# Two decoder layers with a mixture of experts: TensorE's products of the experts' stage pinned to the order of the program

## Chip, cores and metric

One NeuronCore of a Trainium2 chip runs the whole program in one launch. The metric is the device time of one execution in microseconds. A second, profiled execution gives the trace; all stretches below are counted from the start of its span.

## What is computed

512 tokens of width 1024 go through two layers. Each layer has a dense part (norm, one wide projection, three mixers, gated merge, output projection) and then a mixture of experts. A router picks one of four groups and two of its eight experts for each token; all 32 experts of the layer run on the tokens that chose them. The experts' stage is what matters here:

```python
g_sel = jnp.argmax(g_logits, axis=-1)
top_v, top_i = lax.top_k(e_logits, TOP_K)
weights = jax.nn.softmax(top_v, axis=-1) * p_group
...
def expert_block(args):
    xb, e = args
    return (jax.nn.silu(xb @ w_exp_gate[e]) * (xb @ w_exp_up[e])) @ w_exp_down[e]
...
y_rows = y_rows.astype(F32) * row_w[:, None]
out = jax.ops.segment_sum(y_rows, row_tok, num_segments=n_tok + 1)[:n_tok]
```

## The kernel before

`body` runs `dense(l)` and then `moe(l)` for the two layers. In `moe` (from L1059) every expert has a place for 64 tokens (`CAP`). The outer loop runs over eight groups `g` of four experts, the inner loop over two pairs `q` of each group. What TensorE does for a pair, in the order in which the program writes it:

- `expert_up` (L1303) makes the gate and up products of one expert. The 64 tokens' activations are the stationary operand, so a product fills 64 of the array's 128 columns; the two halves `j` of the result go to the two column halves, in turn. One expert is 16 products, which the trace shows as 32 matmuls; it reads four weight blocks of 1 MiB.
- `expert_mid` (L1313) has no large product. ScalarE takes the SiLU (L1317), VectorE multiplies (L1318), TensorE transposes the result in two pieces (L1321) and ScalarE copies it out (L1323). Its tile `h` has one buffer.
- `expert_slots` (L1326) transposes the one-hot matrix of the pair (L1332) and makes the routing weights of its slots (L1336).
- `expert_down` (L1343) makes the down products of both experts of the pair, expert `j` in column half `j`, again in turn (32 matmuls, L1350, four weight blocks). VectorE scales the result (L1356), ScalarE and VectorE split it in two parts (L1357, L1358).
- `back` (L1362) adds the scaled rows back to the tokens: products of a full-width one-hot with both parts (L1371), and a VectorE addition into `x` for each (L1374).
- `gather` (L1277) collects the four experts' tokens of a group: eight parts of eight full-width matmuls (L1290), each copied out by ScalarE (L1292).

The program spreads these over the pairs. In pair `q` = 0 it writes: up of the first expert, half of `back` for the group before, `expert_mid`, up of the second, the other half of `back`, `expert_slots`, `expert_mid`, `expert_down`. In `q` = 1 it writes: two ups, `expert_mid`, `expert_slots`, four parts of the next group's gather, `expert_mid`, `expert_down`, four more parts. Groups 3 and 7 end differently: they have no gather ahead, and `back` follows at once. Between groups 3 and 4 a loop (`extra`, L1428) serves experts with more than 64 tokens.

The weights come through `fetch` (L1170): one transfer of 1 MiB for each block, all issued by SyncE's queue in the order of use, into a ring of twelve places in the first layer and thirteen in the second (nine around the extra loop). A transfer waits until TensorE has finished with the block that had the place before.

The order of instructions on each engine is not written by hand. When the program is built, a scheduler goes through its own estimate of when each instruction's operands are ready and lets each engine take what is ready; the order of the program decides only among those. Data dependencies always hold. PSUM has two buffers for the up products (`mm`), two for the down products (`rt`) and four for everything else (`sm`).

Of the kernel before, what the change touches and what calls it, by code (L numbers as in the profile page):

```python
# [9 lines left out]
F32 = mybir.dt.float32  # L10
# [10 lines left out]
NT = S // 128  # L21
# [154 lines left out]
class Kern:  # L176
# [16 lines left out]
    def c(self, name):  # L193
        o, n = CW[name]
        n1 = CW["i2"][0]
        return self.consts[0][:, o:o + n] if o < n1 else self.consts[1][:, o - n1:o - n1 + n]
# [994 lines left out]
    def route(self, op, rp, lg):  # L1191
# [82 lines left out]

        return pos, late

    def gather(self, oh, n, ahead=3):  # L1277

        nc = self.nc
        l, x, a, b, g2b, xh, xl = self.env  # L1280
        xg = self.xgp.tile([128, 8, 4 * CAP], F32, tag="xg", name="xg")[:, :, :n]
        made = [0]

        def part(k):
            pg = self.psum()[:, :n]
            po = pg.rearrange("p (a s) -> p a s", s=oh.shape[-1])
            i = 0
            for src in (xh, xl):
                for t in range(NT):
                    nc.tensor.matmul(po if len(oh.shape) == 4 else pg, src[:, t, k * 128:(k + 1) * 128], oh[:, t], start=i == 0, stop=i == 7)  # L1290
                    i += 1
            nc.scalar.activation(xg[:, k], pg, AF.Identity, scale=a[:, k:k + 1], bias=b[:, k:k + 1])  # L1292

        def get(k):
            while made[0] < min(8, k + ahead):
                part(made[0])
                made[0] += 1
            return xg[:, k]

        get(0)  # L1300
        return get

    def expert_up(self, xg, wgu):  # L1303

        nc = self.nc
        ph = self.psum("mm")
        for k in range(8):
            for j in range(2):
                nc.tensor.matmul(ph[64 * j:64 * j + 64].rearrange("p (u f) -> p u f", u=2), xg(k),  # L1309
                                 wgu(k)[:, :, 256 * j:256 * j + 256], start=k == 0, stop=k == 7)  # L1310
        return ph

    def expert_mid(self, ph):  # L1313

        nc, c, mp = self.nc, self.c, self.mp
        h = mp.tile([128, 256], F32, tag="h", name="h")
        nc.scalar.activation(h, ph[:, :256], AF.Silu)  # L1317
        nc.vector.tensor_tensor(h, h, ph[:, 256:], op=OP.mult)  # L1318
        pt = self.psum()[:, :256]
        for q in range(2):  # L1320
            nc.tensor.transpose(pt[:, q * 128:(q + 1) * 128], h[:, q * 128:(q + 1) * 128], c("ident"))  # L1321
        hT = mp.tile([128, 2, 2, CAP], F32, tag="hT", name="hT", bufs=3)
        nc.scalar.activation(hT.rearrange("p q j s -> p (q j s)"), pt, AF.Copy)  # L1323
        return hT

    def expert_slots(self, oh, wcol):  # L1326

        nc, c, mp = self.nc, self.c, self.mp
        ohT = mp.tile([128, S], F32R, tag="ohT", name="ohT", bufs=2)
        pt = self.psum()  # L1330
        for t in range(NT):
            nc.tensor.transpose(pt[:, t * 128:(t + 1) * 128], oh[:, t].bitcast(F32), c("ident"))  # L1332
        nc.scalar.activation(ohT, pt, AF.Copy)
        pw = self.psum()
        for t in range(NT):
            nc.tensor.matmul(pw[:, :4], oh[:, t], wcol(t), start=t == 0, stop=t == NT - 1)  # L1336
        ws = self.misc.tile([128, 1], F32, tag="ws", name="ws", bufs=2)
        for j in range(2):
            js = slice(64 * j, 64 * j + 64)
            nc.vector.tensor_reduce(ws[js], pw[js, 2 * j:2 * j + 2], axis=AX.X, op=OP.add)  # L1340
        return ohT, ws

    def expert_down(self, hT, wd, ohT, ws):  # L1343

        nc, g2b = self.nc, self.env[4]
        pys = [self.psum("rt") for _ in range(2)]
        for f in range(4):
            for n in range(2):
                for j in range(2):
                    nc.tensor.matmul(pys[n][64 * j:64 * j + 64], hT[j][:, f % 2, f // 2], wd(j, f)[:, 512 * n:512 * n + 512],  # L1350
                                     start=f == 0, stop=f == 3)
        ys = []
        for n in range(2):
            yh, yl = (self.parts.tile([128, 512], F32R, tag=tag, name=tag, bufs=4) for tag in ("yh", "yl"))
            y = pys[n]
            nc.vector.scalar_tensor_tensor(y, y, ws, g2b[:, n * 512:(n + 1) * 512], op0=OP.mult, op1=OP.mult)  # L1356
            nc.scalar.activation(yh, y, AF.Copy)  # L1357
            nc.vector.tensor_tensor(yl, y, yh.bitcast(F32), op=OP.subtract)  # L1358
            ys.append((yh, yl))
        return ohT, ys  # L1360

    def back(self, done, last=False, blocks=range(NT)):  # L1362

        nc, x = self.nc, self.env[1]
        for t in blocks:
            for n in range(2):
                px = self.psum()
                i = 0
                for ohT, ys in done:
                    for y in ys[n]:  # L1370
                        nc.tensor.matmul(px, ohT[:, t * 128:(t + 1) * 128], y, start=i == 0, stop=i == 2 * len(done) - 1)  # L1371
                        i += 1
                xs = x[:, t, n * 512:(n + 1) * 512]
                nc.vector.tensor_tensor(xs, xs, px, op=OP.add)  # L1374
                if last:
                    nc.scalar.activation(px, xs, AF.Square, accum_out=self.ssx[:, n, t:t + 1])  # L1376
# [162 lines left out]
```

## Time and profile before

| what | value |
|---|---|
| time, median of 3 runs (lowest, highest) | 2514.08 us (2507.03, 2515.6) |
| the profiled execution's own time | 2514.72 us |
| its span, first to last instruction | 2512.9 us |
| PE busy | 2348.6 us, 93% of the span |
| weight loads of TensorE (PEld) busy | 1581.0 us, 63% |
| DVE, ACT busy | 1121.0 us (45%), 657.8 us (26%) |
| matmuls of L1309 and of L1350 with the ring's weights | 2048 and 1024 |
| read from HBM | 568.58 MB |

A group of instructions is named by its line, engine and operation, with the tile that it writes and those that it reads. A matmul's duration in the trace is longer than the distance to the next one, since they overlap; distances are therefore taken from start to start. A bracket at the end of a row of the timeline is the idle time of that engine just before it, and what ended it.

### The profile page before, as it was taken

What the parts mean: (1) busy time and instruction counts of PE and PEld (TensorE: products, weight loads), DVE (VectorE), ACT (ScalarE), POOL (GpSimd) and SP (SyncE); (2) the same over time, 40 slices, a digit from 0 to 9 for tenths busy, and PEclk for the clock granted to TensorE, in tenths of its full rate; (3) what the DMA queues carried; (4) which work ended last, traced back from release to release, by engine and by line L of the source; (5) the groups of instructions that cost most, each with busy time, mean ns of one, the idle gap of its engine ahead of it and who ended that gap; (6) DMA issues with size and microseconds to landing.
All of it is one profiled execution on the core that took longest, in us unless ns stands there. A gap on an engine that the chain in (4) does not pass through costs nothing. (4 is left out here: it accounts for less than half of the span.)

```text
span 2512.9 us, 35831 instructions
## 1 busy us (share of the span) xinstructions
PE 2348.6 (93%) x14542; PEld 1581.0 (63%) x14542; DVE 1121.0 (45%) x2569; ACT 657.8 (26%) x1126; POOL 7.4 (0%) x26
## 2 busy tenths in 40 slices
PE   6999999999979998999989999999999899999997
PEld 4777778777945444554457777787779454445443
DVE  7648665874332122222246477568543322212213
ACT  4323324223321111111143233342233221111111
POOL 0000000000000000000000000000000000000000
PEclk9999999999989999999999999999999899999999
DMA  7222335775459996799942322268453699799993
GB/s 291 63 79 68 86 105 186 258 256 199 150 227 414 360 353 269 323 421 353 347 155 71 85 68 69 100 194 272 161 182 145 239 412 364 302 384 420 394 375 146
DMA packets 139949, 587.22 MB, mean 234 GB/s; under 512 B 37381, under 2 KB 39685, under 8 KB 90629
## 3 DMA queue, kind: packets, MB, share of 16 engines
q1 hardware_dynamic: 136608, 576.44, 61.7%
q10 hardware_dynamic: 3172, 8.45, 1.0%
q8 instruction: 116, 1.90, 0.3%
q14 instruction: 53, 0.43, 0.0%
HBM read 568.58 MB, written 12.06 MB: 231 GB/s over the span
## 5 line engine op out<-in xcount | busy, mean ns | idle before, releaser
L1309 PE MATMUL ps_mm<-w_at,xg_at 128*64 128x512 f32 x2048 | 482.7, 599 | 0.0
L346 PE MATMUL ps_mm<-hTh_at,whi_at 128*128 128x512 f32 x1024 | 414.1, 404 | 10.3 <-DVE b_at L964 4.1
L346 PE MATMUL ps_mm<-hTh_at,wlo_at 128*128 128x512 f32 x1024 | 409.7, 400 | 10.9 <-DVE wlo_at L218 10.9
L346 PE MATMUL ps_mm<-hTl_at,whi_at 128*128 128x512 f32 x1024 | 409.2, 400 | 0.0
L1309 PEld LDWEIGHTS ps_mm<-w_at,xg_at 128*64 128x64 f32 x2048 | 164.5, 136 | 223.6 <-issue 213.0
L217 ACT ACTIVATE whi_at<-raw_at 128x1024 fp32r<-128x1024 f32 (+1 forms) x180 | 170.1, 946 | 471.0 <-PE ps_mm L346 382.5
L218 DVE TENSOR_TENSOR wlo_at<-raw_at,whi_at 128x1024 fp32r<-128x1024 f32 (+1 forms) x180 | 193.9, 1079 | 170.6 <-ACT whi_at L217 157.9
L1350 PE MATMUL ps_rt<-w_at,hT_at 128*64 128x512 f32 x1024 | 253.1, 598 | 0.0
L346 PEld LDWEIGHTS ps_mm<-hTh_at,wlo_at 128*128 128x128 f32 x1024 | 195.7, 191 | 61.9 <-DVE wlo_at L218 18.0
L346 PEld LDWEIGHTS ps_mm<-hTh_at,whi_at 128*128 128x128 f32 x1024 | 195.6, 191 | 53.7 <-issue 7.1
L346 PEld LDWEIGHTS ps_mm<-hTl_at,whi_at 128*128 128x128 f32 x1024 | 195.8, 191 | 43.9 <-issue 4.7
L1356 DVE SCALAR_TENSOR_TENSOR ps_rt<-ps_rt,ws_at,g2b_at 128x512 f32<-128x512 f32 x66 | 50.0, 758 | 280.4 <-PE ps_rt L1350 277.2
L1350 PEld LDWEIGHTS ps_rt<-w_at,hT_at 128*64 128x64 f32 x1024 | 99.4, 136 | 103.1 <-issue 89.2
L1318 DVE TENSOR_TENSOR h_at<-h_at,ps_mm 128x256 f32<-128x256 f32 x65 | 27.3, 421 | 305.8 <-ACT h_at L1317 305.6
L1374 DVE TENSOR_TENSOR x_at<-x_at,ps_sm 128x512 f32<-128x512 f32 x136 | 90.0, 685 | 130.7 <-PE ps_sm L1371 130.4
L1292 ACT ACTIVATE xg_at<-ps_sm,mod_at,mod_a_at 128x256 f32<-128x256 f32 x136 | 76.8, 565 | 181.5 <-PE ps_sm L1290 181.2
L312 DVE SCALAR_TENSOR_TENSOR w_ada_at<-w_ada_at,crow_at 128x1024 f32<-128x1024 f32 x80 | 97.7, 1222 | 52.7 <-DMA w_ada_at<-in_w_ada_dram 52.2
L1371 PE MATMUL ps_sm<-yh_at,ohT_at 128*128 128x512 f32 x264 | 105.9, 415 | 5.7 <-ACT yh_at L1357 3.5
L1371 PE MATMUL ps_sm<-yl_at,ohT_at 128*128 128x512 f32 x264 | 104.2, 411 | 0.4 <-DVE yl_at L1358 0.4
L1317 ACT ACTIVATE h_at<-ps_mm 128x256 f32<-128x256 f32 x65 | 24.9, 384 | 302.6 <-PE ps_mm L1309 302.6
L1290 PE MATMUL ps_sm<-oh_at,xh_at 128*128 128x256 f32 x512 | 95.4, 302 | 6.8 <-DVE oh_at L1105 2.9
L1290 PEld LDWEIGHTS ps_sm<-oh_at,xh_at 128*128 128x128 f32 x512 | 74.3, 198 | 40.3 <-issue 40.3
(373 smaller groups left out, 2995.1 us busy)
## 6 DMA issues: line engine op xcount, KB each, us to landing
w_at<-in_w_exp_dram SPq DMA_DIRECT2D x256, 1024.0 KB, 9.7
w_at<-in_w_down_dram SPq DMA_DIRECT2D x128, 1024.0 KB, 8.1
raw_at<-in_w_in_dram SPq DMA_DIRECT2D x84, 512.0 KB, 3.7
w_ada_at<-in_w_ada_dram SPq DMA_DIRECT2D x80, 512.0 KB, 4.4
raw_at<-in_w_gate_dram SPq DMA_DIRECT2D x48, 512.0 KB, 4.4
raw_at<-in_w_branch_dram SPq DMA_DIRECT2D x48, 256.0 KB, 3.9
w_ada_at<-in_w_ada_dram SPq DMA_DIRECT2D x8, 1024.0 KB, 12.8
raw_at<-in_w_o_dram SPq DMA_DIRECT2D x16, 512.0 KB, 4.8
```

Source lines behind the costliest of these rows:

```text
L217: nc.scalar.activation(hi, src, AF.Copy)
L218: (eng or nc.vector).tensor_tensor(lo, src, hi.bitcast(F32), op=OP.subtract)
L312: nc.vector.scalar_tensor_tensor(w, w, 1.0, self.crow, op0=OP.mult, op1=OP.mult, accum_out=m)
L346: self.nc.tensor.matmul(ps, w[a][:, k], x[b][:, k], start=n == 0, stop=n == last)
L1290: nc.tensor.matmul(po if len(oh.shape) == 4 else pg, src[:, t, k * 128:(k + 1) * 128], oh[:, t], start=i == 0, stop=i == 7)
L1292: nc.scalar.activation(xg[:, k], pg, AF.Identity, scale=a[:, k:k + 1], bias=b[:, k:k + 1])
L1309: nc.tensor.matmul(ph[64 * j:64 * j + 64].rearrange("p (u f) -> p u f", u=2), xg(k), wgu(k)[:, :, 256 * j:256 * j + 256], start=k == 0, st ...
L1318: nc.vector.tensor_tensor(h, h, ph[:, 256:], op=OP.mult)
L1350: nc.tensor.matmul(pys[n][64 * j:64 * j + 64], hT[j][:, f % 2, f // 2], wd(j, f)[:, 512 * n:512 * n + 512], start=f == 0, stop=f == 3)
L1356: nc.vector.scalar_tensor_tensor(y, y, ws, g2b[:, n * 512:(n + 1) * 512], op0=OP.mult, op1=OP.mult)
L1371: nc.tensor.matmul(px, ohT[:, t * 128:(t + 1) * 128], y, start=i == 0, stop=i == 2 * len(done) - 1)
L1374: nc.vector.tensor_tensor(xs, xs, px, op=OP.add)
```

## The change

`Kern` gets two helpers, `mm` and `turn`. They issue a matmul or a transpose and hand it to `keep_in_program_order` of the framework. This ties the instruction behind the last one that was written for the same engine in the same block of the program: an edge of order for the scheduler, without a semaphore and without a wait on the chip. All matmuls and transposes of `gather`, `expert_up`, `expert_mid`, `expert_slots`, `expert_down` and `back` go through the helpers, and since `extra` calls these functions, its products do as well. The order of the other engines' instructions and of the transfers is left to the scheduler. No operand, tile, buffer or count of instructions is changed.

```diff
+    def mm(self, *a, **k):
+
+        self.tc.keep_in_program_order(self.nc.tensor.matmul(*a, **k))
+
+    def turn(self, *a, **k):
+        self.tc.keep_in_program_order(self.nc.tensor.transpose(*a, **k))
...
-                    nc.tensor.matmul(po if len(oh.shape) == 4 else pg, src[:, t, k * 128:(k + 1) * 128], oh[:, t], start=i == 0, stop=i == 7)
+                    self.mm(po if len(oh.shape) == 4 else pg, src[:, t, k * 128:(k + 1) * 128], oh[:, t], start=i == 0, stop=i == 7)
...
-                nc.tensor.matmul(ph[64 * j:64 * j + 64].rearrange("p (u f) -> p u f", u=2), xg(k),
+                self.mm(ph[64 * j:64 * j + 64].rearrange("p (u f) -> p u f", u=2), xg(k),
...
-            nc.tensor.transpose(pt[:, q * 128:(q + 1) * 128], h[:, q * 128:(q + 1) * 128], c("ident"))
+            self.turn(pt[:, q * 128:(q + 1) * 128], h[:, q * 128:(q + 1) * 128], c("ident"))
...
-            nc.tensor.transpose(pt[:, t * 128:(t + 1) * 128], oh[:, t].bitcast(F32), c("ident"))
+            self.turn(pt[:, t * 128:(t + 1) * 128], oh[:, t].bitcast(F32), c("ident"))
...
-            nc.tensor.matmul(pw[:, :4], oh[:, t], wcol(t), start=t == 0, stop=t == NT - 1)
+            self.mm(pw[:, :4], oh[:, t], wcol(t), start=t == 0, stop=t == NT - 1)
...
-                    nc.tensor.matmul(pys[n][64 * j:64 * j + 64], hT[j][:, f % 2, f // 2], wd(j, f)[:, 512 * n:512 * n + 512],
+                    self.mm(pys[n][64 * j:64 * j + 64], hT[j][:, f % 2, f // 2], wd(j, f)[:, 512 * n:512 * n + 512],
...
-                        nc.tensor.matmul(px, ohT[:, t * 128:(t + 1) * 128], y, start=i == 0, stop=i == 2 * len(done) - 1)
+                        self.mm(px, ohT[:, t * 128:(t + 1) * 128], y, start=i == 0, stop=i == 2 * len(done) - 1)
```

## Rows read from the trace of the kernel before

**Rows 1.** The page: its head, the busy times, and the largest group (out<-in, count, busy us, mean ns of one).

```profile
span 2512.9 us, 35831 instructions
PE 2348.6 (93%) x14542; PEld 1581.0 (63%) x14542; DVE 1121.0 (45%) x2569; ACT 657.8 (26%) x1126; POOL 7.4 (0%) x26
L1309 PE MATMUL ps_mm<-w_at,xg_at 128*64 128x512 f32 x2048 | 482.7, 599 | 0.0
```

**Rows 2.** Busy times by stretch; the stretches run from the first up product of a second pair (`q` = 1) to that of the next, or to the end of the last `back`. Columns: stretch, its length, busy us and count of PE, PEld, DVE, ACT and POOL, granted TensorE clock, DMA share, GB/s.

```profile
740.99:803.39 62.40, 62.40 (x317) 34.38 (x315) 14.86 (x29) 10.75 (x22) 0.00 (x0) 1.00 1.01 416
803.39:872.45 69.06, 65.19 (x315) 32.07 (x313) 14.70 (x29) 11.18 (x22) 0.00 (x0) 1.00 0.94 365
...
941.51:976.26 34.75, 32.06 (x143) 15.55 (x139) 14.54 (x39) 4.73 (x10) 0.00 (x0) 1.00 0.91 361
1048.72:1113.31 64.59, 64.58 (x317) 33.29 (x314) 14.85 (x29) 10.75 (x22) 0.00 (x0) 1.00 1.01 420
...
1251.45:1287.88 36.43, 32.62 (x143) 15.54 (x140) 13.23 (x26) 9.71 (x22) 1.07 (x2) 1.00 0.51 193
1995.66:2058.03 62.37, 62.37 (x317) 34.36 (x315) 14.87 (x29) 10.75 (x22) 0.00 (x0) 1.00 1.01 416
2058.03:2125.50 67.47, 65.14 (x314) 32.42 (x312) 14.69 (x29) 11.18 (x22) 0.00 (x0) 1.00 0.96 369
...
2194.56:2229.34 34.78, 32.09 (x143) 15.56 (x139) 12.52 (x23) 4.52 (x9) 0.00 (x0) 1.00 0.93 389
2261.55:2326.14 64.59, 64.58 (x316) 33.29 (x314) 14.85 (x29) 10.75 (x22) 0.00 (x0) 1.00 1.01 421
...
2395.20:2464.27 69.07, 65.20 (x315) 32.05 (x312) 13.23 (x25) 11.18 (x22) 0.00 (x0) 1.00 0.95 368
2464.27:2500.42 36.15, 32.49 (x143) 15.45 (x139) 11.00 (x19) 8.45 (x21) 0.00 (x0) 1.00 0.19 72
```

**Rows 3.** Timeline of PE from 742.28 to 803.39 us of the span, one row for each of nine places in it. Columns: start us, us, engine, line, operation, out<-in, shape, count.

```profile
742.28 14.01 PE L1309 MATMUL ps_mm<-w_at,xg_at 128*64 128x512 f32 x61
756.22 0.44 PE L1321 MATMUL ps_sm<-consts_at,h_at 128*128 128x128 f32 x2
...
761.53 7.86 PE L1350 MATMUL ps_rt<-w_at,hT_at 128*64 128x512 f32 x32
769.33 0.74 PE L1290 MATMUL ps_sm<-oh_at,xh_at 128*128 128x256 f32 x4
...
773.34 7.09 PE L1309 MATMUL ps_mm<-w_at,xg_at 128*64 128x512 f32 x32
780.36 0.50 PE L1371 MATMUL ps_sm<-yh_at,ohT_at 128*128 128x512 f32 x1
...
784.17 0.38 PE L1321 MATMUL ps_sm<-consts_at,h_at 128*128 128x128 f32 x2
...
796.10 0.44 PE L1321 MATMUL ps_sm<-consts_at,h_at 128*128 128x128 f32 x2
...
803.39 0.59 PE L1309 MATMUL ps_mm<-w_at,xg_at 128*64 128x512 f32 x1
```

**Rows 4.** First the waits of PE in the stretch 803.39 to 872.45 us (engine, tile, line, releaser: us in total, times, longest), then the timeline of PE at five places of the same stretch.

```profile
PE ps_sm L1321 <- DVE h_at L1318: 3.9, 4, 1.0
...
811.95 0.44 PE L1321 MATMUL ps_sm<-consts_at,h_at 128*128 128x128 f32 x2 [0.99 <-DVE h_at L1318]
...
837.36 1.94 PE L1350 MATMUL ps_rt<-w_at,hT_at 128*64 128x512 f32 x8
839.23 0.50 PE L1371 MATMUL ps_sm<-yl_at,ohT_at 128*128 128x512 f32 x1
839.57 0.40 PE L1371 MATMUL ps_sm<-yh_at,ohT_at 128*128 128x512 f32 x1
839.80 0.39 PE L1371 MATMUL ps_sm<-yl_at,ohT_at 128*128 128x512 f32 x1
```

**Rows 5.** Timeline of PE in the extra loop and in group 4: the first products of a `back` that follows its down products at once, and two ups in a row with the transposes behind them.

```profile
1009.78 0.49 PE L1371 MATMUL ps_sm<-yh_at,ohT_at 128*128 128x512 f32 x1 [0.63 <-ACT yh_at L1357]
1010.64 0.50 PE L1371 MATMUL ps_sm<-yh_at,ohT_at 128*128 128x512 f32 x1 [0.36 <-ACT yh_at L1357]
...
1026.26 13.95 PE L1309 MATMUL ps_mm<-w_at,xg_at 128*64 128x512 f32 x64
1040.14 0.44 PE L1321 MATMUL ps_sm<-consts_at,h_at 128*128 128x128 f32 x2
...
1042.29 0.44 PE L1321 MATMUL ps_sm<-consts_at,h_at 128*128 128x128 f32 x2
```

**Rows 6.** The weights' stream: its issues on the page (count, size, median us from issue to landing), a stretch of 20 us in which it runs without pause (columns as in rows 2), the waits of SyncE's queue from 740 to 1290 us, and the idle time of PE and PEld that a block of weights ended before L1309 in the whole span (us, times).

```profile
w_at<-in_w_exp_dram SPq DMA_DIRECT2D x256, 1024.0 KB, 9.7
...
1040.00:1060.00 20.00, 20.00 (x97) 9.40 (x97) 3.95 (x8) 3.11 (x7) 0.00 (x0) 1.00 1.01 423
...
SPq L1179 <- PE ps_mm L1309: 236.0, 104, 8.6
...
  DMA w_at<-in_w_exp_dram: 3.1, 10
```

**Rows 7.** Timeline of ACT and DVE behind an up product of the stretch 740.99 to 803.39 us (idle time before, and what ended it, in brackets).

```profile
780.54 0.39 ACT L1317 ACTIVATE h_at<-ps_mm 128x256 f32<-128x256 f32 x1 [6.52 <-PE ps_mm L1309]
...
780.96 0.42 DVE L1318 TENSOR_TENSOR h_at<-h_at,ps_mm 128x256 f32<-128x256 f32 x1 [9.41 <-ACT h_at L1317]
```

## Prediction

> **What bounds the kernel now.** Read the page first [rows 1]: TensorE is busy for 93% of the span and the up products of the experts are its largest group, so the end moves only if TensorE gets through its list sooner. A busy share over the whole span cannot tell whether the list itself can be passed faster, so the next view is the table of stretches [rows 2]. I cut the experts' stage into laps, from the first up product of a second pair to that of the next. Each lap contains every step of a group once: four ups, four sets of transposes, two down products, one gather, one `back`, 24 weight blocks. The reader is to see that laps of the same work differ: the first lap of each layer takes 62.4 us, the first one after the extra loop 64.59 us, one 67.47 us, and seven take 69.06 to 69.08 us (the first and the last of the seven are shown). In the short laps PE is busy throughout; in the long ones it is idle for 3.9 of 69.06 us [rows 2, 4].
>
> The timeline says what the difference is. In the first lap [rows 3] the order of TensorE is that of the program (three products at its beginning overlap the down product before): two ups in a row, transposes, slots and gather, transposes, the whole down product (32 matmuls), the rest of the gather, an up of 32, half of `back`, transposes, and so on. In the next lap [rows 4] the same work is chopped: a down product runs in pieces of eight (one weight block), with pieces of gather or `back` between, and transposes stand directly behind the up that they depend on. So the first lap already is the changed kernel, as far as TensorE's order goes, measured on the chip.
>
> **The price of the chopped order.** Two terms, which should add up to the difference of laps.
> - The transposes wait for ScalarE's SiLU and VectorE's product: four waits in a lap, 3.9 us in all, 0.99 us for the one shown [rows 4].
> - Each change between half-width and full-width products costs time. A piece of eight takes 1.87 us from its start to the next full-width product (837.36 to 839.23), where eight of a long run take 13.88 x 8/64 = 1.74 us (1026.26 to 1040.14) [rows 4, 5]; the full-width product behind it takes 0.34 us where the one after takes 0.23 us [rows 4]. With some 0.1 us on the way back (an estimate, as large as the step just read) that is about 0.3 us for a piece. By a count in the timeline the long lap has some 12 pieces more than the first: about 3.6 us.
>
> Together 7.5 us, and the laps differ by 69.06 - 61.6 = 7.46 us (next part). Nothing is left over that a third cause would have to explain.
>
> **A lap in the order of the program.** From the transposes at 756.22 to the next lap's first product at 803.39 it is 47.17 us [rows 3]. Ahead of these stand two ups: the first takes 811.95 - 0.99 - 803.39 = 7.57 us when it follows a down product whose second column half lags [rows 3, 4], the second 13.88 - 7.02 = 6.86 us (the pair of ups, less one of 773.34 to 780.36) [rows 3, 5]. Sum 47.17 + 7.57 + 6.86 = 61.6 us. (The first lap's 62.4 us begin earlier inside a down product; I leave it as it is.)
>
> **What the change adds.** The edges issue nothing on the chip. What they cost is that TensorE no longer takes other work where the next product's operand is late. Behind a product that waits now stands the whole rest of the stage on TensorE, and SyncE's queue, whose next place comes free only when TensorE goes on. Three places:
> - *Transposes.* In a lap their operand is hidden: behind an up, SiLU and product end about 1.0 us after the next TensorE instruction starts (780.36 to 781.38) [rows 3, 7], and half a `back` (3.81 us, 780.36 to 784.17) or slots and gather stand between. I take 0. If that cover failed everywhere, it is 0.99 us each [rows 4], four times in ten changed laps, 40 us.
> - *The down product.* It starts behind its last transposes, and its second column half waits for ScalarE's copy. That is why it takes 7.80 us (761.53 to 769.33) where 32 matmuls take 7.02 [rows 3]. It is inside the 61.6 us. If it vanished, ten laps would gain 8 us; I take no gain.
> - *The ends of groups 3 and 7.* No gather stands between, so the second transposes come 2.15 us after the first (1040.14 to 1042.29), as measured where the program has the same sequence [rows 5]. Then 0.3 us of transposes, 7.80 us of down product and 32 products of `back`: 2 x 3.81 us [rows 3], and 0.63 + 0.36 us of waiting for the split parts, as behind the extra loop [rows 5]. With both ups: 14.43 + 2.15 + 0.3 + 7.8 + 8.6 = 33.3 us, against 34.75, 36.43, 34.78 and 36.15 us [rows 2]. Its unknown is the waiting: between 0 and 2 us each, plus or minus 4 us over the four.
>
> The extra loop, and the beginnings of both halves, keep their lengths: there the products stood in program order or had nothing else to run.
>
> **The stream of weights** must follow, or the gain is given back. A lap needs 24 x 1.0486 = 25.17 MB. Without pause the stream brings 423 GB/s, 416 over the whole first lap [rows 2, 6]: 59.5 to 60.5 us, less than 61.6. In the long laps it runs at 365 GB/s, but not by itself: SyncE's queue waits for TensorE to give places back, 236 us in total in the first layer [rows 6]. Twelve places are half a lap, about 30 us, and a transfer takes 9.7 us from issue to landing [rows 6], so there is room for a burst of two ups. TensorE lost 3.1 us to late blocks of up weights in the whole span [rows 6]. I take 0; the bound is half of the way back to 69.06 us, 3.7 us a lap, 37 us in all. The room is small: at 61.6 us the stream is in use for 97% of the time.
>
> A rule of the Trainium skill speaks against this. Its page "DMA: Bandwidth & Descriptors", section "Bandwidth", says that between HBM and SBUF the HBM side binds at about 358 GB/s for a core. By that a lap could not be shorter than 70.3 us, and the change would do nothing. The stretch at 423 GB/s [rows 6] contradicts it here, where one core runs alone, and the same page has a measurement of 425 GB/s.
>
> **The sum.** Seven laps: 7 x 7.46 = 52.2 us. The lap of 67.47: 5.9 us. The two of 64.59, which should become like the first, 62.4: 4.4 us. The four ends: 142.1 - 4 x 33.3 = 8.9 us. Together 71.4 us. The profiled execution took 2514.72 us (span 2512.9 and 1.8 around it), 0.6 us above the median of the runs: 2514.7 - 71.4 = 2443 us.
>
> **Rivals.**
> 1. *The stream binds.* If the 365 GB/s of the long laps are its own limit, the chopping only followed the arriving blocks and the laps stay at 69 us: 2515 us, no change. For it: pieces of eight are one block each, and 97% leaves little. Against it: 416 GB/s over a full lap with PE never idle, and a queue that waits for TensorE. In between, with laps of 66 to 68 us, 2485 to 2505 us.
> 2. *Nothing is reordered.* The edges tie TensorE's instructions only; if the scheduler kept its order all the same, 2515 us. An edge between each product and the one before leaves it no choice, so this is unlikely; I count it with the first.
> 3. *The waits come back in TensorE's queue.* Place: VectorE's queue, whose order is still chosen by the scheduler's estimate. If it puts the additions of `back` (L1374) ahead of the product for `h` (L1318), the transposes wait until TensorE's own `back` is through and the chain behind it, up to the 2.15 us of the uncovered case [rows 5], forty times in ten laps: 86 us, 2443 + 86 = 2529 us, slower. It decides from 71.4/40 = 1.8 us at each. For it: TensorE cannot step aside any more. Against it: VectorE works 14.9 of 62.4 us [rows 2], and in the first lap its product for `h` came 0.4 us behind SiLU's start [rows 7].
>
> **How the numbers follow.** About 0.3%, 7.5 us, can be told from no change. Forecast (2431 to 2480 us): 0.83. Below it 0.02. The stream binds in part (2480 to 2506): 0.04. No change by rivals 1 or 2: 0.06. Slower by rival 3: 0.05. So faster 0.89, same 0.06, slower 0.05. The range goes down by the 8 us of the down product and the 4 us of the ends, and up by 37 us, nearly the 40 us of either unknown alone, since both at once would need two things to fail.
>
> **What the profile after would show.** Right: all laps at 61 to 62.5 us, down products and ups in unbroken runs of 32, no wait of L1321 inside a lap, stream at 405 to 420 GB/s, ends of 33 us. Wrong by rival 1: PE idle in front of L1309 or L1350, ended by a weights' transfer, with the stream at a DMA share of 1. Wrong by rival 3: waits of L1321 on L1318 of over 1 us in every lap, with L1374 ahead of L1318 on DVE. Wrong by rival 2: pieces of eight as before. The forecast fails altogether if the first lap owes its length to blocks loaded ahead rather than to its order.

## The result and the profile after

The changed kernel takes 2437.64 us (median; 2435.43 to 2443.56) against 2514.84 us for the kernel before in the same job: a ratio of 0.970, with an interval of 0.967 to 0.973. The forecast was 2443 us. It was worked out from one profiled execution, and the profiled execution of the changed kernel took 2443.56 us. That the two agree to 1 us is luck: when the changed kernel was run again (below), its executions took 2430.93 to 2461.88 us.

The page after: its head, the busy times, and the group of the up products, which the matmul helper (L1279) now records ([rows 1] before).

```profile
span 2441.8 us, 35867 instructions
PE 2310.8 (95%) x14542; PEld 1636.8 (67%) x14542; DVE 1122.7 (46%) x2569; ACT 654.2 (27%) x1126; POOL 7.4 (0%) x26
L1279 PE MATMUL ps_mm<-w_at,xg_at 128*64 128x512 f32 x2048 | 459.9, 594 | 0.0
```

The number of matmuls is the same, and so is that of every other operation. The 36 instructions more in the head are semaphore instructions, which the busy times leave out: the trace has 55 more in TensorE's queue and 19 fewer in those of VectorE and ScalarE. So the count of instructions did change a little. PE's busy time is 38 us shorter, and its share rose. So the gain has two halves: about half of the 71 us was idle time, and half was time in which the page called PE busy.

The stretches after, cut as in [rows 2] and with the same columns: a lap of each half of the first layer, the last lap, and the four ends.

```profile
799.09:860.62 61.53, 61.53 (x315) 35.80 (x313) 14.80 (x29) 10.75 (x22) 0.00 (x0) 1.00 1.00 411
...
922.14:954.84 32.70, 31.39 (x143) 18.86 (x139) 14.70 (x39) 4.52 (x10) 0.00 (x0) 1.00 0.89 361
1026.34:1087.88 61.54, 61.54 (x315) 35.85 (x313) 14.77 (x29) 10.76 (x22) 0.00 (x0) 1.00 1.01 421
...
1210.93:1244.75 33.82, 31.41 (x143) 19.02 (x140) 14.06 (x27) 10.47 (x23) 1.07 (x2) 1.00 0.64 230
...
2145.00:2178.00 33.00, 31.53 (x143) 18.89 (x139) 12.86 (x24) 4.31 (x9) 0.00 (x0) 1.00 0.98 410
...
2334.06:2395.60 61.54, 61.54 (x315) 35.81 (x313) 13.46 (x25) 10.76 (x22) 0.00 (x0) 1.00 1.01 421
2395.60:2429.27 33.67, 31.71 (x143) 18.80 (x139) 11.43 (x20) 8.65 (x21) 0.00 (x0) 1.00 0.30 121
```

All twelve laps now have one length, 61.51 to 61.54 us, where [rows 2] had four lengths from 62.4 to 69.1 us. PE is busy from end to end in each.

Timeline of PE in the second lap, the one that was chopped in [rows 4].

```profile
799.52 14.01 PE L1279 MATMUL ps_mm<-w_at,xg_at 128*64 128x512 f32 x63
813.46 0.44 PE L1282 MATMUL ps_sm<-consts_at,h_at 128*128 128x128 f32 x2
...
818.46 0.38 PE L1282 MATMUL ps_sm<-consts_at,h_at 128*128 128x128 f32 x2
818.76 7.86 PE L1279 MATMUL ps_rt<-w_at,hT_at 128*64 128x512 f32 x32
826.56 0.74 PE L1279 MATMUL ps_sm<-oh_at,xh_at 128*128 128x256 f32 x4
...
830.57 7.09 PE L1279 MATMUL ps_mm<-w_at,xg_at 128*64 128x512 f32 x32
837.59 0.50 PE L1279 MATMUL ps_sm<-yh_at,ohT_at 128*128 128x512 f32 x1
...
841.40 0.38 PE L1282 MATMUL ps_sm<-consts_at,h_at 128*128 128x128 f32 x2
841.71 7.09 PE L1279 MATMUL ps_mm<-w_at,xg_at 128*64 128x512 f32 x32
```

The reader is to see runs of 32 and 63 half-width products, and no bracket on any row. (The first matmul of the 64 stands just ahead, before the last one of a down product.) With this the second rival of the prediction, that nothing is reordered, has fallen. Behind the up that ends at 837.59 SiLU and the product for `h` run while TensorE is in `back`; here ACT, then DVE, in that stretch (two timelines).

```profile
837.77 0.39 ACT L1324 ACTIVATE h_at<-ps_mm 128x256 f32<-128x256 f32 x1 [6.52 <-PE ps_mm L1279]
```

```profile
838.18 0.42 DVE L1325 TENSOR_TENSOR h_at<-h_at,ps_mm 128x256 f32<-128x256 f32 x1 [9.41 <-ACT h_at L1324]
838.84 0.69 DVE L1381 TENSOR_TENSOR x_at<-x_at,ps_sm 128x512 f32<-128x512 f32 x1 [0.23 <-PE ps_sm L1279]
```

VectorE takes the product for `h` ahead of the additions of `back`, so `h` is there at 838.60 us and the transposes are due at 841.40. From the first lap to the end of group 3 two waits are left, both in that end. All waits of PE in this stretch:

```profile
PE ps_sm L1282 <- DVE h_at L1325: 1.0, 1, 1.0
PE ps_sm L1279 <- DVE yl_at L1365: 0.3, 1, 0.3
```

### The profile page after: what moved, and what is told of

Same layout as the page of the kernel before. It is cut to its first block, busy times and chain, and to the rows that moved or that the text cites. A ratio compares the mean times of both kernels' runs of the same rounds, so it can differ in the third digit from the quotient of the medians.

```text
span 2441.8 us, 35867 instructions
## 1 busy us (share of the span) xinstructions
PE 2310.8 (95%) x14542; PEld 1636.8 (67%) x14542; DVE 1122.7 (46%) x2569; ACT 654.2 (27%) x1126; POOL 7.4 (0%) x26
## 3 DMA queue, kind: packets, MB, share of 16 engines
q1 hardware_dynamic: 136608, 576.44, 62.4%
## 5 line engine op out<-in xcount | busy, mean ns | idle before, releaser
L1279 PE MATMUL ps_mm<-w_at,xg_at 128*64 128x512 f32 x2048 | 459.9, 594 | 0.0
L1279 PEld LDWEIGHTS ps_mm<-w_at,xg_at 128*64 128x64 f32 x2048 | 198.8, 137 | 225.0 <-issue 217.6
L1279 PE MATMUL ps_rt<-w_at,hT_at 128*64 128x512 f32 x1024 | 246.8, 595 | 0.0
L1279 PEld LDWEIGHTS ps_rt<-w_at,hT_at 128*64 128x64 f32 x1024 | 115.2, 137 | 104.1 <-issue 88.0
L1279 PE MATMUL ps_sm<-yl_at,ohT_at 128*128 128x512 f32 x264 | 104.4, 396 | 3.5 <-DVE yl_at L1365 3.5
L1279 PE MATMUL ps_sm<-yh_at,ohT_at 128*128 128x512 f32 x264 | 107.1, 406 | 0.6 <-ACT yh_at L1364 0.6
L1364 ACT ACTIVATE yh_at<-ps_rt 128x512 fp32r<-128x512 f32 x66 | 39.5, 598 | 242.4 <-DVE ps_rt L1363 242.4
L1279 PE MATMUL ps_sm<-oh_at,xh_at 128*128 128x256 f32 x512 | 90.0, 300 | 6.9 <-DVE oh_at L1105 2.9
```

What stands on the lines that cost most here:

```text
L1279: self.tc.keep_in_program_order(self.nc.tensor.matmul(*a, **k))
```

## The experiments

The theory of the prediction has two prices: 0.99 us for transposes that stand directly behind their up, and about 0.3 us for each run of half-width products that is cut off from the next (a piece). Its rivals are that only one of the two counts, and that the weights' stream had set the old laps. In the diffs a line of "..." leaves code out. Lengths of laps are from the profiles, read as above. Laps of one order repeat to 0.05 us within a profile, while the executions of one kernel differ by 6 to 31 us.

**The price of a piece alone.** The second up of a first pair and the down product of a second pair are cut in quarters, the first up in two quarters and a half: eight pieces more in a lap. Parts of `back` stand between those of the ups, parts of the gather between those of the down product, all tied to the order of the program. (`between` writes one group of `back` in `expert_up`, one part of the gather in `expert_down`.)

```diff
...
                                  wgu(k)[:, :, 256 * j:256 * j + 256], start=k == 0, stop=k == 7)
+            if between and k % 2:
+                between(k // 2)
...
                                      start=f == 0, stop=f == 3)
+            if between:
+                between(f)
...
```

> All tied, no transpose moved closer to its up, but the program itself cuts the products: quarters of the two ups of a first pair alternate with back, quarters of the down product of a second pair with the gather. 8 more half-width pieces in every lap and no waits. Theory of two prices: 8 x 0.3 = 2.4 us more, laps of 63.9 us, twelve of them, about 2466 us. If a change of width cost nothing and only waits counted: 61.5 us and 2438 us. If the even supply of weights helped: below 61.5.

2473.61 us, and all twelve laps 64.30 to 64.32 us. A lap and five rows of its timeline, from its down product:

```profile
863.84:928.14 64.30, 64.30 (x314) 34.05 (x312) 15.62 (x35) 10.73 (x22) 0.00 (x0) 1.00 0.97 391
```

```profile
883.52 2.71 PE L1283 MATMUL ps_rt<-w_at,hT_at 128*64 128x512 f32 x8
886.16 0.74 PE L1283 MATMUL ps_sm<-oh_at,xh_at 128*128 128x256 f32 x4
...
887.30 1.94 PE L1283 MATMUL ps_rt<-w_at,hT_at 128*64 128x512 f32 x8
889.17 0.74 PE L1283 MATMUL ps_sm<-oh_at,xh_at 128*128 128x256 f32 x4
...
890.32 1.94 PE L1283 MATMUL ps_rt<-w_at,hT_at 128*64 128x512 f32 x8
```

PE never waits in this lap, and the page would call all of it busy. Eight pieces cost 64.30 - 61.53 = 2.77 us, 0.346 us each. None of this was won back at the down product: its first eight matmuls still lag, with 2.64 us from start to start (883.52 to 886.16) where the next eight take 1.87. That a piece costs nothing has fallen.

**The price of a wait alone.** Two versions. In the first the program writes each expert's transposes directly behind its up; in the second it only writes the second transposes of a pair a little earlier. In both the down product starts with its operand copied, so that their difference is the waits and one piece. The diff of the first stands ahead of its expectation, then that of the second (`covered` is true in a first pair that has a `back`).

```diff
...
+                    if prev or q:
+                        hT.append(self.expert_mid(ph[j]))
                     if prev:
                         self.back(prev, False, (2 * j, 2 * j + 1))
-                        if not j:
-                            hT.append(self.expert_mid(ph[0]))
...
```

> All tied as in the change, but the program writes each expert's transposes directly behind its up. Four waits of 0.99 us and one more half-width piece in a lap, less about 1.0 us, since the down product's second column half is now covered by slots and gather: 61.5 + 3.96 + 0.3 - 1.0 = 64.8 us a lap, twelve laps, about 2480 us in all. To be compared with the version that only covers the down product. If TensorE made up for the waits later (waits without a price), laps of 60.5 to 61.5 us.

```diff
...
+                if covered:
+                    hT.append(self.expert_mid(ph[1]))
                 at_slots = self.expert_slots(ohp, wcol)
                 if ahead:
-                    nxg = self.gather(nxt_oh.rearrange("p t e s -> p t (e s)"), 4 * CAP, 4)
-                hT.append(self.expert_mid(ph[1]))
+                    nxg = self.gather(nxt_oh.rearrange("p t e s -> p t (e s)"), 4 * CAP, 3)
+                if not covered:
+                    hT.append(self.expert_mid(ph[1]))
+                if ahead:
+                    nxg(1)
...
```

> The change, and the second transposes of a pair are written earlier: before the slots in a first pair, before the last part of the gather in a second pair, so that ScalarE's copy is done when the down product begins. Nothing else moves. If the lag of the down product's second column half is that copy: 0.77 us (7.79 to 7.02) and about 0.23 us less in a lap, 60.5 us, twelve laps, about 2426 us. If the stream of weights sets a floor: no lap under 59.5 to 60.5 us, and idle time of TensorE ended by weights. If the lag has another cause: 61.5 us and 2438 us.

First version: 2477.59 us, laps of 64.42 to 64.45 us, and 64.95 to 64.99 us for the first of each half. Its waits in one lap:

```profile
PE ps_sm L1283 <- DVE h_at L1326: 3.9, 4, 1.0
```

Second version: 2424.61 us (ratio to before 0.965, interval 0.9623 to 0.9677), laps of 60.13 us, and 60.67 us for the first of each half. A lap, and its down product, which took 818.76 to 826.56 above, 7.80 us from start to start, and takes 820.69 to 827.71, 7.02 us, here:

```profile
801.56:861.69 60.13, 60.13 (x314) 29.81 (x312) 14.81 (x29) 10.76 (x22) 0.00 (x0) 1.00 1.01 420
```

```profile
820.69 7.09 PE L1285 MATMUL ps_rt<-w_at,hT_at 128*64 128x512 f32 x32
827.71 0.74 PE L1285 MATMUL ps_sm<-oh_at,xh_at 128*128 128x256 f32 x4
```

Between the versions lie 64.43 - 60.13 = 4.30 us: 3.9 us of waits and one piece of 0.346 make 4.25. So each price stands by itself. The gain of covering the down product was 1.4 us where I expected 1.0: the 0.78 us seen here, and the rest at the other down product and around the transposes.

**Parts of the change.** Only the transposes tied, then only the products.

```diff
-        self.tc.keep_in_program_order(self.nc.tensor.matmul(*a, **k))
+        self.nc.tensor.matmul(*a, **k)
...
-        self.tc.keep_in_program_order(self.nc.tensor.transpose(*a, **k))
+        self.nc.tensor.transpose(*a, **k)
```

> Only the transposes are tied behind what the program writes before them; the products are left to the scheduler. In a lap of its order the products still stand in 7 more half-width pieces than in the program's order, and one transpose stands close behind its up. Theory of two prices (0.3 us for a piece, 0.99 us for a transpose behind its up): 7 x 0.3 + 0.5 = 2.6 us more than 61.5, laps of 64.1 us, five of six in a layer, about 2466 us. If the waits were the whole cause: laps of about 62 us, 2442 us. If the weights' stream had set the old laps: 69 us as before.

> Only the products are tied; the transposes are left to the scheduler, which sets two of four in a lap directly behind their up, and through the gap the second up is cut: 4 more pieces. Theory of two prices: 4 x 0.3 + 2 x 0.99 = 3.2 us more, laps of 64.7 us in eight of twelve, about 2463 us. If pieces cost nothing: laps of 63.5 us. If waits cost nothing that is not given back elsewhere: 62.7 us.

Only the products: 2477.51 us (profiled span 2464.3). The first lap of each half keeps the 61.5 us of the change, as expected; of the other eight, seven take 64.62 to 64.64 us and one, where no transposes wait, 62.55 us. A lap of 64.63 us and its waits:

```profile
863.90:928.53 64.63, 62.70 (x314) 34.32 (x312) 15.72 (x35) 11.05 (x22) 0.00 (x0) 1.00 0.97 388
```

```profile
PE ps_sm L1282 <- DVE h_at L1325: 1.9, 2, 1.0
```

1.9 + 4 x 0.346 = 3.3 us, and 3.10 were measured: as expected. Only the transposes: 2481.11 us where I expected about 2466. Four laps of six in a layer take 65.78 us, not five of six at 64.1; the first lap of each half keeps the length that it had before the change. 65.78 us is 1.7 us a lap more than I expected. The one wait of its lap is 0.87 us and the timeline has six more pieces, 2.1 us. The largest part of the rest is at a place that I had counted as a piece like the others:

```profile
907.47 1.07 PE L1279 MATMUL ps_mm<-w_at,xg_at 128*64 128x512 f32 x2
908.47 0.44 PE L1282 MATMUL ps_sm<-consts_at,h_at 128*128 128x128 f32 x2
908.84 1.93 PE L1279 MATMUL ps_mm<-w_at,xg_at 128*64 128x512 f32 x6
```

The transposes stand after two matmuls, so between the products of the two column halves for the same part of the operand. The pieces of two and six take 1.00 + 1.86 us where eight take 1.87: 0.99 us more. (That the column halves are the reason was not tried.) 0.87 + 2.08 + 0.99 = 3.94 of 4.25 us; 0.3 us stay unexplained. Either half of the change alone gives about half of the gain.

**The third rival on purpose.** VectorE's product for `h` and its additions of `back` are tied too.

```diff
-        nc.vector.tensor_tensor(h, h, ph[:, 256:], op=OP.mult)
+        self.tc.keep_in_program_order(nc.vector.tensor_tensor(h, h, ph[:, 256:], op=OP.mult))
...
-                nc.vector.tensor_tensor(xs, xs, px, op=OP.add)
+                self.tc.keep_in_program_order(nc.vector.tensor_tensor(xs, xs, px, op=OP.add))
```

> The change, and VectorE's product for h and its additions of back are tied to the order of the program as well, so that in a first pair the product for h stands behind the additions of half a back. This is the third rival made on purpose. The last addition ends about 1.0 us after the last product of the half, the product for h takes 0.42 us more: the first transposes wait about 1.5 us, the second, with the slots of 0.8 us between, about 0.7 us. 2.2 us a lap, laps of 63.7 us, twelve of them, about 2464 us. By the rival's own price, 2.15 us each: 65.8 us and 2490 us. If VectorE's slack hides it: 61.5 us.

2461.28 us, laps of 63.85 us. DVE, then PE, where the first transposes are late (timelines):

```profile
904.20 0.69 DVE L1381 TENSOR_TENSOR x_at<-x_at,ps_sm 128x512 f32<-128x512 f32 x1 [0.22 <-PE ps_sm L1279]
904.80 0.41 DVE L1325 TENSOR_TENSOR h_at<-h_at,ps_mm 128x256 f32<-128x256 f32 x1
```

```profile
905.27 0.44 PE L1282 MATMUL ps_sm<-consts_at,h_at 128*128 128x128 f32 x2 [1.11 <-DVE h_at L1325]
```

The mechanism is real, 2.3 us a lap. But it hits only the two transposes of a lap that have a `back` ahead of them, at 1.11 and 0.87 us (I had expected 1.5 and 0.7), not four at 2.15; 0.3 us of the lap are not in these waits. So the rival's price of 86 us was three to four times too high. It would have left the change at 2461 us, faster than before all the same.

**The stream.** Nine places in the ring; less work for TensorE, since the gather takes the high part alone; both.

```diff
-        n = len(SB_RING) if self.nload in self.narrow else len(self.ring)
+        n = len(SB_RING)
...
-            for src in (xh, xl):
+            for src in (xh,):
...
```

> The change with nine places for weights everywhere in place of twelve and thirteen. If the stream has room in the order of the program because twelve places carry it over three products in a row (96 matmuls, 21 us, twelve blocks, while 8 to 9 arrive), nine should just do, or cost up to 1 us a lap: 61.5 to 62.5 us, up to 2450 us. If the order of the program needs the whole ring: TensorE waits for up weights in every lap and the laps are 64 us or more, over 2468 us.

> The change, with the low part left out of every gather (products of xl, 32 of 64 matmuls of a group's gather; the gathered values lose their low bits). TensorE's work in a lap falls by 3.9 us to 57.6 us. If the stream of weights is the next bound: laps of 59.5 to 60.5 us with idle time of TensorE ended by weights, and a DMA share of 1. If it is not: 57.6 us. The three other gathers of a layer (the first, that of the extra loop, that of the second half) get shorter by some 3.9 us each in either case.

> As the run without the gathers' low part (left out here too), with nine places for weights everywhere. There the stream ran without pause at 420 to 422 GB/s, 24.3 MB in a lap of 57.69 us that needs 25.17 MB, so the stock in the ring fell by 0.8 block a lap, and only the last lap of each half waited for weights. If that stock is what hid the stream's limit, three places less bring the waits into the first or second lap and the laps then go to 25.17 MB / 421 GB/s = 59.8 us. If the stream had been sped up by the shorter work, the laps stay at 57.7 us.

Nine places: 2446.43 us, laps of 61.53 to 61.54 us, none longer than in the change. High part only: 2379.64 us. I expected laps of 59.5 to 60.5 us, and they are 57.69; only the last lap of each layer is longer (58.23 and 58.46). Two laps of the first layer's second half, and PE's and SyncE's waits from 736 to 1220 us ([rows 6] have SyncE's of before):

```profile
1063.63:1121.32 57.69, 57.69 (x283) 31.96 (x280) 14.99 (x30) 10.16 (x22) 0.00 (x0) 1.00 1.01 421
1121.32:1179.55 58.23, 57.90 (x282) 31.32 (x280) 13.58 (x27) 10.15 (x22) 0.00 (x0) 1.00 1.01 420
```

```profile
PE ps_mm L1279 <- DMA w_at<-in_w_exp_dram: 3.0, 4, 1.1
```

```profile
SPq L1179 <- PE ps_mm L1279: 105.3, 68, 6.5
SPq L1179 <- DMA w_at<-in_w_exp_dram: 90.4, 50, 2.2
```

Of PE's 3.0 us 0.34 are in the longer lap and 2.6 behind it, in the end of group 7.

The stream did not get faster: 420 to 422 GB/s at a DMA share of 1.01 in the laps of the first layer, which is 25.17 MB in 59.8 us. The difference of 2.1 us a lap was paid from the stock in the ring. By the transfers' landings and the starts of the products that use them, the first block of groups 1, 2 and 3 had landed 14.5, 12.6 and 10.7 us ahead of its use: 1.9 us less each time. With nine places the same figures are 7.8, 4.8 and 2.9 us. That version took 2395.44 us in its one execution. Its laps are 57.7 us too, and the last one of each layer 59.29 and 60.08 us. (The expectation says that the last lap of each half waited; it was that of each layer.) So the stock hides the limit and falls as expected, but I placed the waits too early: the first half of a layer has three laps, 6 us of stock, and nine places hold that; the second half begins with nine places in either kernel.

**The change again, and fewer pieces.** The third version also writes the whole gather ahead of the second pair's down product, and both ups of a first pair ahead of `back`, so that a lap has two half-width runs of 96 matmuls. The diff is against the second version (the lines taken out are in the loop over the two ups, those added behind it).

```diff
...
-                    if prev:
-                        self.back(prev, False, (2 * j, 2 * j + 1))
-                        if not j:
-                            hT.append(self.expert_mid(ph[0]))
...
+                if prev:
+                    self.back(prev, False, (0, 1))
+                hT.append(self.expert_mid(ph[0]))
+                if prev:
+                    self.back(prev, False, (2, 3))
...
-                    nxg(1)
+                    nxg(5)
```

> The change itself once more, beside the two versions below. Laps of 61.5 us and about 2438 us. The stretch between the end of the first layer and the first gather of the second, which was 672.4 us before and 679.6 us after, has been 669 to 685 us in the runs since: if that is variation of a run, it comes out within these bounds, not at 679.6 us.

> The version with the covered down product once more, beside the change on the same chip: laps of 60.67 and 60.13 us, and by its laps 4 x 0.87 + 8 x 1.41 = 14.8 us less than the change.

> As the version with the covered down product; besides, the whole gather is written before the down product of a second pair, and both ups of a first pair stand ahead of back, so that a down product and the two ups behind it are one half-width run twice a lap: two such runs in a lap where that version has four. By the price measured in the chopped version, (64.30 - 61.54) / 8 = 0.345 us for each: 60.13 - 0.69 = 59.44 us a lap, 12 x 0.69 = 8 us less in all, about 2416 us. If only the waits were worth anything: 60.13 us. If the stream (59.8 us for a lap without pause) binds at once: no lap under 59.8 us, with idle time of TensorE ended by weights.

The change again 2436.25 us, the covered version 2422.24 us (ratio 0.9655, interval 0.9633 to 0.9677), the third 2419.61 us (0.9621, 0.9602 to 0.9641). A lap of the third:

```profile
862.05:921.48 59.43, 59.43 (x315) 29.88 (x313) 15.53 (x35) 10.75 (x22) 0.00 (x0) 1.00 1.01 421
```

59.40 to 59.44 us, and 59.96 for the first of a half: 0.70 us less than the covered version in each, as 2 x 0.346 forecast. One of its runs of 96, a down product and the two ups behind it:

```profile
825.61 7.09 PE L1284 MATMUL ps_rt<-w_at,hT_at 128*64 128x512 f32 x32
832.53 13.90 PE L1284 MATMUL ps_mm<-w_at,xg_at 128*64 128x512 f32 x64
```

The 32 matmuls of the down product take 6.92 us from start to start when the ups follow, and 7.02 us when full-width products do (820.69 to 827.71 above). So going on to other operands and another PSUM tile has no price here. That speaks for the change of width as what is paid at the end of a run; why it costs anything is not shown. Over twelve laps the 0.70 us are 8.5 us; the medians differ by 2.6 us, and the intervals overlap, so by whole runs alone the third version is not told from the second. Both beat the change. The stream runs without pause, and its 59.8 us are longer than the lap: it lives on the stock, and less work on TensorE would soon bring nothing.

## Why the prediction was right, step by step

| step | predicted | measured in the profile |
|---|---|---|
| a lap in the order of the program | 61.6 us | 61.51 to 61.54 us |
| seven laps of 69.06 | -52.2 us | -52.7 us |
| the lap of 67.47 | -5.9 us | -5.9 us |
| two laps of 64.59 | -4.4 us | -4.5 us: -6.1 us, and +1.6 us at the beginnings of the halves |
| four ends | 4 x 33.3 us, -8.9 us | 32.70, 33.82, 33.00, 33.67 us, -8.9 us |
| first laps, with the beginnings of the layers | 0 | +1.5 us: -1.7 us, and +3.2 us at the beginnings |
| the extra loop | 0 | -1.8 us |
| outside the stage | 0 | +1.2 us (-5.9 and +7.2) |
| sum | -71.4 us | -71.2 us of span |

The laps and the ends, which carry the sum, came out as forecast. That the sum agrees to 0.2 us is luck: the last three terms above it were put at nothing and came out at +1.5, -1.8 and +1.2 us.

- *The first lap as a measurement of the changed kernel.* Right. It carried 63 of the 71 us, and the doubt at the end of the prediction, that this lap owed its length to blocks loaded ahead, has fallen: twelve laps have its length, with nine places as well as with twelve.
- *The price of the chopped order.* Right in kind, and the sum of 7.5 us fits 69.06 - 61.53 = 7.53, but two errors cancel in it. A piece costs 0.346 us, not 0.3, so twelve cost 4.15 us and the two terms make 8.05. Against that the old order covered part of the lag of the second pair's down product: its first eight matmuls took 2.16 us there (826.63 to 828.79 in the trace of before) against 1.87 for other eights, 0.29 us of lag where the program's order has 0.77. 8.05 - 0.48 = 7.57. "Nothing is left over" was right by luck.
- *Transposes at no cost.* Right inside the laps: no wait there, and 0.96 to 0.99 us at each end, as in the sum. At the beginnings of the halves, which the prediction left as they were, there is one (below).
- *The down product.* The gain of 8 us that I named and did not take was there to be had, but by another change than this one, and it was larger: 14.8 us by the laps (4 x 0.87 + 8 x 1.41).
- *The ends.* The sum is exact, its parts are not: the waiting for the split parts was 0.32 us in group 3 of both layers, 1.45 and 0.99 us in group 7, where I put 0.99 each.
- *The stream.* Right that it follows. In eleven of the twelve laps it moved 409 to 421 GB/s, and 343 in the third lap of the second layer; a lap needs 25.17 MB in 61.53 us, 409 GB/s, which is 97% of 421. No product of a lap waits for weights, so the first rival, that the stream had set the old laps, has fallen. My bound of 37 us was too wide: even with nine places the laps kept their length. The Trainium skill's page "DMA: Bandwidth & Descriptors", section "Bandwidth", gives about 358 GB/s for each core when both cores of an HBM domain stream, and 425 GB/s measured on a core alone. The prediction took the first figure for a rule against this kernel; with one core at work, the last version's 421 GB/s over a whole lap agrees with the second.
- *Beginnings and extra loop keep their lengths.* Not quite. At each of the four beginnings TensorE now waits 0.87 or 0.88 us for transposes that it could step around before, and at the first it ran at a granted clock of 0.91 for 0.95. The extra loop's gather ran at a higher clock than before (below). The beginnings' 4.8 us are nearly made up by the loop's 1.8 us and by the four first laps, together 3.4 us shorter than in the sum: in the kernel before they had begun earlier, inside a down product.
- *Outside the stage.* The -5.9 us (ahead of the first layer's stage) and +7.2 us (between the stages) are not shown to be the change's. From the last product of the first layer to the first gather of the second it was 672.4 us before and 679.6 after; the change again had 671.0, and the eleven other profiles lie between 663.8 and 685.5 us. The edit ties nothing in the dense parts. In the trace some 60 to 80 of the 4690 matmuls of the second layer's dense part stand at another place of TensorE's order than before, in both profiles of the changed kernel; these two are 8.6 us apart, so no effect of that order is shown. That is also the size of what separates two runs of one kernel, and why laps, not medians, decide the small questions here.

## What to carry to other kernels

If laps of equal work have different lengths in one profile, the shortest is a measurement of what the order of work can give; take the forecast from it, and look in the longer ones for what is cut and what waits. It need not be the limit: two further versions came to 60.13 and 59.43 us. A busy share of 100% does not mean that an engine's list is passed at its best speed: each half-width run more among full-width products cost 0.35 us here and counted as busy. Fix the order on the engine that is the bottleneck, and be slow to tie the engines that feed it: here tying two of VectorE's operations as well gave back a third of the gain.

## What was not expected of the hardware

A half-width run that was cut between the products of its two column halves cost 0.99 us, in eight laps of one version; one that was cut behind a pair cost 0.346 us. And the same gather of 64 matmuls at the start of the extra loop took 9.36 us before and 7.87 us after. The stretches, before and then after (columns as in [rows 2]):

```profile
978.36:987.72 9.36, 9.36 (x65) 9.22 (x65) 2.36 (x19) 3.95 (x7) 0.00 (x0) 0.82 0.01 3
```

```profile
956.94:964.81 7.87, 7.87 (x65) 7.74 (x65) 2.36 (x19) 3.95 (x7) 0.00 (x0) 1.00 0.15 61
993.71:1003.09 9.38, 9.38 (x65) 9.25 (x65) 0.00 (x0) 3.96 (x7) 0.00 (x0) 0.82 0.87 339
```

The granted clock was 0.82, so partly at the lower level of 1.2 GHz, and 1.00, so at 2.4 GHz throughout. In both kernels TensorE had idled 1.94 us directly before; the `back` ahead of it had waited 0.63 us more in the kernel before and 0.32 us in the one after. That difference does not decide. The version with only the transposes tied had the wait of 0.63 us and took 7.87 us at 1.00. The chopped version had 0.32 us, as after, and took as long as before:

```profile
962.94:972.30 9.36, 9.36 (x65) 9.22 (x65) 2.36 (x19) 3.96 (x7) 0.00 (x0) 0.82 0.16 64
```

At the end of the loop the same gather is at 0.82 in both kernels (the last row of the one after; before, 1016.97 to 1026.26, 9.29 us). What decides stays open; the 1.5 us were no part of the forecast.
